# Stick-breaking attention: the causal mask moved from GpSimd, on the scores, to VectorE, where the transposed weights leave PSUM

## The chip, the cores and the metric

The kernel runs on one core of one Trainium2 chip. The metric is the device time of one execution in microseconds (us), which ends with the last instruction of the core. A core has four engines that compute: TensorE (PE in the profile, with its weight loads as PEld), VectorE (DVE), ScalarE (ACT) and GpSimd (POOL). SyncE (SP) issues the DMAs. Each engine works through its own list of instructions in order, and semaphores make it wait for the others.

## What is computed

One layer of a streaming encoder: a normalised input goes through one large projection; two mixers (stick-breaking attention and RWKV-7) read it; their outputs are projected, gated, merged and projected again. The change is in the attention, 16 heads of 64 columns, 512 prompt tokens and 8 streams of 16 new tokens:

```
def _sb_attend(q, k, v, q_pos, k_pos):
    """A[t,s] = beta[t,s] * prod_{s<j<t} (1 - beta[t,j]), beta = sigmoid(q.k/sqrt(d)), s < t only."""
    z = einsum('bhqd,bhkd->bhqk', q, k) * (D_HEAD_A ** -0.5)
    valid = k_pos[None, :] < q_pos[:, None]
    log_keep = where(valid, log_sigmoid(-z), 0.0)
    later = cumsum(log_keep, axis=3, reverse=True) - log_keep
    weight = where(valid, exp(log_sigmoid(z) + later), 0.0)
    return einsum('bhqk,bhkd->bhqd', weight, v)
```

The prompt is swept in four blocks of 128 queries; block i reads keys 0 to 128(i+1)-1. Only the last 128 keys of a block need the mask `s < t`, a 128 by 128 triangle.

## The kernel before

The matrix products of the projections are a long list of jobs of 128 output columns each (`gemm_range`). A job is two halves of eight steps, and a step is three matmuls of 320 columns (`xh·whi`, `xl·whi`, `xh·wlo`: float32 as a high and a low part). The order of jobs is: the projections that the RWKV mixer needs, mixed with those of the attention; then eight jobs for the gate gB; then eight with the weight w_o_b (called oB here), whose input is the RWKV output, reloaded into `xh` and `xl` as soon as the last gB step has read each slice (`reload`, lines 1542 to 1567: GpSimd copies a slice `xh<-rl`, VectorE forms `xl<-rl,xh`); then eight with w_o_a (oA), which needs all of the attention; then the output projection.

The attention works on eight head pairs, one after the other (`attn`, line 1294), with a preparation `aprep` of the next pair running beside it. For a pair there are nine items: the sampled streams ("s") and then, for query blocks 3, 2, 1, 0, the two heads. An item has three parts, which are staggered:

- `score`: two matmuls into a bank `ps_a`; ScalarE makes `kp` = sigmoid(-z/8) and `bt` = sigmoid(z/8); GpSimd multiplies the last 128 columns of `bt` by the triangle `see` (line 1340); VectorE scans `kp` into the running product from the right (with `stop` as the data that stands for the mask), and multiplies `bt` by it (line 1345).
- `flip`, two items later: TensorE transposes `bt` into a bank `ps_b` (two of these, shared with the transposes of `aprep`), and ScalarE copies it to `wt`.
- `pv`, once both heads of a query block are flipped: `wt` times the values into the one bank `ps_c`. For "s", the result is gated by `sg<-ps_c,sg` on VectorE, whose factor GpSimd makes (`sg<-sg,sz`), before the bank is given to the prompt's blocks.

What stands when on each engine is decided while the program is built: attention, preparation and reloads are generators, a planner (`Driver`, `Clock`, `_Eng`) keeps an estimated time for each engine, and the jobs' steps are put wherever no generator is ready by that estimate. Its costs for the two operations of this change are

```
            elif e == "dve":
                d = 0.075 + n * 0.00106
            elif e == "pool":
                d = 0.2 + n * (0.0022 if op == "tensor_tensor" else 0.0012)
```

so with n = 128 it reckons 0.48 us for the mask on GpSimd and 0.21 us for one on VectorE. A change in `score` or `flip` therefore also moves the jobs' steps.

Of the kernel before, what the change touches and what calls it, by code (L numbers as in the profile page):

```python
# [29 lines left out]
AF = mybir.ActivationFunctionType  # L30
ALU = mybir.AluOpType
# [22 lines left out]
def make_consts():  # L54
    r = np.arange(128)
    out = {}
    out["ident"] = np.eye(128)
    none = np.zeros((128, 128))
    see = (r[None, :] < r[:, None]).astype(float)
    out["see"] = see  # L60
    out["stop"] = np.concatenate([none, none, none, 1.0 - see], axis=1)
    for g in range(2):
        b = 4 * g + r[:, None] // 32
        t = r[:, None] % 16
        bb, s = r[None, :] // 16, r[None, :] % 16
        out[f"mnew{g}"] = np.where((b == bb) & (s < t), 0.0, -1e30)
    s = r[:, None] % 64
    t = r[None, :] % 64
    strict = r[None, :] < 64
    caus = np.where(strict, s < t, s <= t)  # L70
    out["maskp"] = caus.astype(float)
    out["masks"] = (caus & (s // 16 == t // 16)).astype(float)
    out["bones"] = (r[:, None] // 64 == r[None, :] // 64).astype(float)
    tok = np.arange(640)
    first = np.where(tok < 512, tok % 64 == 0, tok % 16 == 0)
    out["rmask"] = np.broadcast_to(np.where(first, 0.0, 1.0), (128, 640))
    out["msk4"] = ((r[:, None] % 64) // 16 == np.arange(4)[None, :]).astype(float)
    return np.ascontiguousarray(np.concatenate(
        [out[n] for n in CONST_COLS] + [out[n] for n in MASK_COLS], axis=1).astype(np.float32))
# [262 lines left out]
def body(tc, ins, outs, dbg=None):  # L342
# [24 lines left out]
    def take(which, *need, hold=False):  # L367


        while True:  # L370
            yield [which, *need]
            old = clk.replaced(which)
            if old not in held:
                break
            yield lambda: old not in held
        t = bank(which)
        if hold:
            held.add(_name(t))
        return t
# [16 lines left out]
    act = clk.wrap("act", nc.scalar).activation  # L396
# [25 lines left out]
    def vtt(out, in0, in1, op):  # L422
        V.tensor_tensor(out=out, in0=in0, in1=in1, op=op)

    def gtt(out, in0, in1, op):
        G.tensor_tensor(out=out, in0=in0, in1=in1, op=op)
# [867 lines left out]
    def attn(p):  # L1294
# [4 lines left out]
        stop, see = ap["msk"][:, 0:512], ap["msk"][:, 512:640]  # L1299
# [7 lines left out]
        def score(it):  # L1307
            ps = yield from take("a")
            kp = ap["as2"].tile([128, 512], F32, tag="kp", name="kp", bufs=2)
            bt = ap["as2"].tile([128, 512], F32, tag="bt", name="bt", bufs=4)  # L1310
            if it[0] == "s":
                qbd = o["qbd"]
                for g in range(2):
                    for i in range(4):
                        mm(ps[32 * i:32 * i + 32, g * 256:g * 256 + 128],
                           lhsT=qbd[:, 4 * g + i].rearrange("p h t -> p (h t)"),
                           rhs=KT[:, 4 * g + i, :], start=True, stop=True)
                    d = ps[:, g * 256 + 128:g * 256 + 256]
                    mm(d, lhsT=qbd[:, 4 * g:4 * g + 4].rearrange("p b h t -> p (b h t)"),
                       rhs=o["kT"][:, 512:640], start=True, stop=False)  # L1320
                    mm(d, lhsT=identb, rhs=mnew[g], start=False, stop=True)
                act(out=kp, in_=ps, func=AF.Sigmoid, scale=-0.125)
                act(out=bt, in_=ps, func=AF.Sigmoid, scale=0.125)
                bv = bt.rearrange("p (g s) -> p g s", g=2)
                for g in range(2):
                    c = slice(g * 256, (g + 1) * 256)
                    V.tensor_tensor_scan(out=kp[:, c][:, ::-1], data0=kp[:, c][:, ::-1],
                                         data1=stop[:, 0:256],
                                         initial=1.0, op0=ALU.mult, op1=ALU.add)
                kv = kp.rearrange("p (g s) -> p g s", g=2)  # L1330
                vtt(bv[:, :, 0:255], bv[:, :, 0:255], kv[:, :, 1:256], ALU.mult)
            else:
                _, i, h = it
                n = 128 * (i + 1)
                qs = slice(128 * i, 128 * i + 128)
                mm(ps[:, :n], lhsT=o["qh"][:, h, qs], rhs=o["ks"][:, h, :n], start=True, stop=False)
                mm(ps[:, :n], lhsT=o["ql"][:, h, qs], rhs=o["ks"][:, h, :n], start=False, stop=True)
                act(out=kp[:, :n], in_=ps[:, :n], func=AF.Sigmoid, scale=-0.125)
                act(out=bt[:, :n], in_=ps[:, :n], func=AF.Sigmoid, scale=0.125)
                gtt(bt[:, n - 128:n], bt[:, n - 128:n], see, ALU.mult)  # L1340
                kv = kp[:, :n]
                V.tensor_tensor_scan(out=kv[:, ::-1], data0=kv[:, ::-1],
                                     data1=stop[:, 512 - n:][:, ::-1],
                                     initial=1.0, op0=ALU.mult, op1=ALU.max)
                vtt(bt[:, 0:n - 1], bt[:, 0:n - 1], kp[:, 1:n], ALU.mult)
            return bt

        def flip(it, bt):
            m = 4 if it[0] == "s" else it[1] + 1
            ps = yield from take("b")  # L1350
            for i in range(m):
                tp(ps[:, i * 128:(i + 1) * 128], bt[:, i * 128:(i + 1) * 128], ident)
            wt = ap["as2"].tile([128, 512], F32, tag="wt", name="wt")
            act(out=wt[:, :m * 128], in_=ps[:, :m * 128], func=AF.Copy)
            return wt

        vt, Vp = tok["v"], o["Vp"]
# [37 lines left out]
        for n in range(len(seq) + 3):  # L1395
            if n < len(seq):
                bts[n] = yield from score(seq[n])
                if n == 0:
                    setf("sc0", p)
                if n == len(seq) - 1:  # L1400
                    setf("scored", p)
                yield []
            m = n - 2
            if 0 <= m < len(seq):
                yield [bts[m]]
                wts[m] = yield from flip(seq[m], bts.pop(m))
            m = n - 3
            if m == 0:
                yield [wts[0]]
                yield from pv(seq[0], [wts.pop(0)])  # L1410
            elif m > 0 and m % 2 == 0:
                yield [wts[m - 1], wts[m]]
                yield from pv(seq[m], [wts.pop(m - 1), wts.pop(m)])
# [366 lines left out]
```

## Time and profile before

| what | us |
|---|---|
| median of 3 runs (1156.38 to 1159.37) | 1158.27 |
| the profiled execution, its own time | 1159.46 |
| its span, first to last instruction | 1157.7 |
| busy in the span: PE | 1107.9 |
| busy in the span: DVE | 751.0 |
| busy in the span: ACT | 630.9 |
| busy in the span: POOL | 392.1 |

The attention lies between about 735 and 960 us of the span. The jobs' steps fill TensorE between its pieces, so that TensorE is busy nearly all of the time, and what the kernel can lose or gain without a change of TensorE's own work is TensorE's idle time: 1157.7 - 1107.9 = 49.8 us in the whole span. Nearly every operation is recorded by one helper line (L214), so groups are told apart by the names of their tiles.

### The profile page before, as it was taken

The numbers are of one execution on the slowest core, as the hardware profiler recorded it, in microseconds if no ns is written. First come the engines' busy times: TensorE is split into PE (matmuls) and PEld (weight loads), VectorE is DVE, ScalarE is ACT, GpSimd is POOL, SyncE is SP. The second block draws the span as 40 slices with busy tenths as digits, with TensorE's granted clock in tenths as the row PEclk, the third lists the DMA queues.
The fourth block names the chain that finished last, engine by engine and source line by source line (L and its number), as shares of the span: only waits on it lengthen the run. The fifth ranks groups of instructions, "written<-read, shape, count | busy, mean of one in ns | idle before, by whom it ended". The sixth has DMA issues, their size and how long they took to land. (4 is left out here: it accounts for less than half of the span.)

```text
span 1157.7 us, 25429 instructions
## 1 busy us (share of the span) xinstructions
PE 1107.9 (96%) x10050; PEld 1034.6 (89%) x10050; DVE 751.0 (65%) x1517; ACT 630.9 (54%) x1347; POOL 392.1 (34%) x605
## 2 busy tenths in 40 slices
PE   6999999999999999999999999998998998999997
PEld 4989899999999999899898999987887787999997
DVE  6487875855967778777783533577767775535324
ACT  5636466485595775858756465555555551123123
POOL 3030706234161361513615021445445434103302
PEclk9999999999999999999999999999999999999999
DMA  5222222233132142222323244966677525354412
GB/s 194 79 82 73 69 74 67 77 100 110 39 112 73 56 118 61 79 72 57 112 68 90 95 118 135 265 182 180 181 216 202 148 72 161 111 163 141 146 47 91
DMA packets 205294, 130.70 MB, mean 113 GB/s; under 512 B 78332, under 2 KB 184696, under 8 KB 205176
## 3 DMA queue, kind: packets, MB, share of 16 engines
q1 hardware_dynamic: 204888, 129.03, 37.9%
q8 instruction: 79, 1.29, 0.5%
q14 instruction: 39, 0.32, 0.1%
q0 software_dynamic: 288, 0.05, 0.0%
HBM read 97.70 MB, written 31.35 MB: 111 GB/s over the span
## 5 line engine op out<-in xcount | busy, mean ns | idle before, releaser
L214 PE MATMUL ps_g<-xh,whi 128*128 128x320 f32 (+1 forms) x1424 | 468.9, 329 | 1.1 <-ACT xh L214 1.1
L214 PE MATMUL ps_g<-xl,whi 128*128 128x320 f32 (+1 forms) x1424 | 443.0, 311 | 4.6 <-DVE xl L214 4.6
L214 PE MATMUL ps_g<-xh,wlo 128*128 128x320 f32 (+1 forms) x1424 | 442.2, 311 | 1.1 <-DVE wlo L214 1.1
L214 PEld LDWEIGHTS ps_g<-xh,whi 128*128 128x128 f32 x1424 | 270.5, 190 | 8.7 <-issue 3.4
L214 PEld LDWEIGHTS ps_g<-xl,whi 128*128 128x128 f32 x1424 | 270.4, 190 | 8.2 <-DVE xl L214 6.5
L214 PEld LDWEIGHTS ps_g<-xh,wlo 128*128 128x128 f32 x1424 | 269.5, 189 | 2.2 <-DVE wlo L214 2.2
L214 DVE TENSOR_TENSOR wlo<-raw,whi 128x1024 fp32r<-128x1024 f32 x97 | 123.9, 1277 | 71.3 <-ACT whi L214 70.5
L214 ACT ACTIVATE whi<-raw 128x1024 fp32r<-128x1024 f32 x97 | 102.5, 1056 | 82.3 <-PE ps_g L214 55.7
L214 DVE TENSOR_TENSOR_SCAN kp<-kp,amsk 128x256 f32<-128x256 f32 (+3 forms) x80 | 73.7, 930 | 31.6 <-ACT kp L214 31.4
L214 POOL TENSOR_TENSOR bt<-bt,amsk 128x128 f32<-128x128 f32 x64 | 44.7, 702 | 117.0 <-ACT bt L214 98.5
L214 ACT ACTIVATE kp<-ps_a 128x512 f32<-128x512 f32 (+3 forms) x72 | 33.1, 459 | 60.4 <-PE ps_a L214 31.7
L214 ACT ACTIVATE sp<-ps_g 128x320 f32<-128x320 f32 x80 | 35.0, 438 | 52.9 <-PE ps_g L214 42.6
L214 POOL TENSOR_TENSOR itmp<-INV 128x28 f32<-128x28 f32 (+6 forms) x112 | 46.5, 415 | 39.4 <-DVE INV L214 32.0
L214 ACT ACTIVATE RH<-ps_b 128x128 f32<-128x128 f32 (+1 forms) x64 | 19.4, 303 | 69.2 <-PE ps_b L214 69.0
L214 DVE SCALAR_TENSOR_TENSOR X<-ps_b,wc,SW 64x64 f32<-64x64 f32 x96 | 27.0, 282 | 45.7 <-PE ps_b L214 44.4
L214 ACT ACT_TABLE_LOAD x39 | 50.0, 1283 | 10.9 <-DVE BK L214 7.6
L214 POOL TENSOR_TENSOR wl<-wd,wh 128x256 fp32r<-128x256 f32 x8 | 7.2, 905 | 134.0 <-issue 109.1
L214 PE MATMUL ps_b<-cst,bt 128*128 128x128 f32 x192 | 33.8, 279 | 15.8 <-DVE bt L214 14.8
L214 DVE TENSOR_TENSOR bt<-bt,kp 128x511 f32<-128x511 f32 (+4 forms) x72 | 43.6, 605 | 8.2 <-POOL bt L214 0.6
L214 POOL TENSOR_TENSOR INV<-INV,itmp 128x28 f32<-128x28 f32 (+6 forms) x112 | 45.9, 410 | 8.8
L214 POOL TENSOR_TENSOR ux<-X,cst 128x256 f32<-128x256 f32 x32 | 20.3, 653 | 75.6 <-PE ps_b L214 44.7
L214 PE MATMUL ps_g<-olo,mgh 128*128 128x256 f32 x160 | 45.0, 281 | 0.0
(252 smaller groups left out, 2346.2 us busy)
## 6 DMA issues: line engine op xcount, KB each, us to landing
raw<-in_w_in_dram SPq DMA_DIRECT2D x81, 512.0 KB
q<-dr_q SPq DMA_DIRECT2D x32, 160.0 KB
Kr<-in_cache_sb_k_dram SPq DMA_DIRECT2D x16, 256.0 KB
Vp<-in_cache_sb_v_dram SPq DMA_DIRECT2D x16, 256.0 KB
raw<-in_w_o_b_dram SPq DMA_DIRECT2D x8, 512.0 KB
raw<-in_w_o_a_dram SPq DMA_DIRECT2D x8, 512.0 KB
oraw<-in_w_out_dram SPq DMA_DIRECT2D x4, 1024.0 KB
dr_zB<-zm SPq DMA_DIRECT2D x8, 320.0 KB
```

The costliest lines, as they stand in the source:

```text
L214: r = f(*a, **k)
```

## The change

The mask is taken out of `score`. In `flip`, ScalarE copies only the blocks of the transposed weights that need no mask (none for query block 0), and VectorE multiplies the last block by the transposed triangle while it moves it from PSUM to `wt`. The constant `see` is stored transposed. "s" items are as before. VectorE's scan keeps its own mask (`stop`).

```
-    out["see"] = see
+    out["see"] = see.T
...
                 act(out=bt[:, :n], in_=ps[:, :n], func=AF.Sigmoid, scale=0.125)
-                gtt(bt[:, n - 128:n], bt[:, n - 128:n], see, ALU.mult)
                 kv = kp[:, :n]
...
             wt = ap["as2"].tile([128, 512], F32, tag="wt", name="wt")
-            act(out=wt[:, :m * 128], in_=ps[:, :m * 128], func=AF.Copy)
+            if it[0] == "s":
+                act(out=wt, in_=ps, func=AF.Copy)
+            else:
+                d = slice((m - 1) * 128, m * 128)
+                if m > 1:
+                    act(out=wt[:, :d.start], in_=ps[:, :d.start], func=AF.Copy)
+                vtt(wt[:, d], ps[:, d], see, ALU.mult)
             return wt
```

So 64 GpSimd operations go (8 pairs, 8 prompt items each) and 64 on VectorE come; of ScalarE's 64 copies of prompt items, 16 go and 48 get shorter by 128 columns.

The orders of the two built programs differ in three places of interest. All are taken from the seventh pair.

VectorE, from the first item of query block 2 on (`kp<-kp,amsk` is the scan, which the profile calls TENSOR_TENSOR_SCAN; `ks<-kT,ks` belongs to the next pair's preparation). Before:

```order
L214 SCALAR_TENSOR_TENSOR kp<-kp,amsk 128x384
L214 TENSOR_TENSOR bt<-bt,kp 128x383
L214 TENSOR_TENSOR sg<-ps_c,sg 128x128
L214 SCALAR_TENSOR_TENSOR kp<-kp,amsk 128x384
L214 TENSOR_TENSOR bt<-bt,kp 128x383
L214 SCALAR_TENSOR_TENSOR kp<-kp,amsk 128x256
L214 TENSOR_TENSOR bt<-bt,kp 128x255
L214 TENSOR_TENSOR ks<-kT,ks 64x512 x2
```

The same place in the changed program:

```order
L214 SCALAR_TENSOR_TENSOR kp<-kp,amsk 128x384
L214 TENSOR_TENSOR bt<-bt,kp 128x383
L214 TENSOR_TENSOR ks<-kT,ks 64x512 x2
L214 TENSOR_TENSOR wt<-ps_b,amsk 128x128
L214 TENSOR_TENSOR sg<-ps_c,sg 128x128
L214 SCALAR_TENSOR_TENSOR kp<-kp,amsk 128x384
L214 TENSOR_TENSOR bt<-bt,kp 128x383
L214 TENSOR_TENSOR wt<-ps_b,amsk 128x128
L214 SCALAR_TENSOR_TENSOR kp<-kp,amsk 128x256
L214 TENSOR_TENSOR bt<-bt,kp 128x255
```

The mask of block 3's first head (`wt<-ps_b,amsk`) stands behind the next pair's two `ks` operations, which have moved up, and the mask of its second head behind one more scan and product.

TensorE, at the transposes of block 2's first head (`ps_b<-cst,bt 128x128 x3`), which need the product `bt<-bt,kp 128x383` above, and at block 3's `pv` (`ps_c<-wt,vtok 64x128 x8`), which needs both masks. Before:

```order
L214 MATMUL ps_b<-cst,bt 128x128 x4
L214 MATMUL ps_a<-ks,qh 128x256
L214 MATMUL ps_a<-ks,ql 128x256
L214 MATMUL ps_b<-cst,bt 128x128 x3
L214 MATMUL ps_g<-xh,whi 128x320
L214 MATMUL ps_g<-xl,whi 128x320
L214 MATMUL ps_g<-xh,wlo 128x320
L214 MATMUL ps_g<-xh,whi 128x320
L214 MATMUL ps_g<-xl,whi 128x320
L214 MATMUL ps_g<-xh,wlo 128x320
L214 MATMUL ps_c<-wt,vtok 64x128 x8
```

In the changed program four steps stand between the `ps_a<-ks,ql 128x256` and the transposes, and four between the transposes and `pv`; the last of the first four and the first of the second four are

```order
L214 MATMUL ps_g<-xh,whi 128x320
L214 MATMUL ps_g<-xl,whi 128x320
L214 MATMUL ps_g<-xh,wlo 128x320
L214 MATMUL ps_b<-cst,bt 128x128 x3
L214 MATMUL ps_g<-xh,whi 128x320
L214 MATMUL ps_g<-xl,whi 128x320
L214 MATMUL ps_g<-xh,wlo 128x320
```

Counted over the whole attention, from the first transposes of `Kr` to the last `pv`, 205 steps of the jobs stood between its pieces, and 277 do now; 88 of those with `xh` are left behind it, where 160 were. The change to the oB jobs, with its reload of `xh` and `xl`, so falls into the seventh pair's attention, where it stood behind the eighth's. TensorE's instructions are otherwise the same ones.

GpSimd, in the seventh pair, from the next pair's `ks` on. Before:

```order
L214 TENSOR_SCALAR ks<-kT 64x512 x2
L214 TENSOR_TENSOR bt<-bt,amsk 128x128
L214 TENSOR_TENSOR sg<-sg,sz 128x640
L214 TENSOR_TENSOR bt<-bt,amsk 128x128 x2
L214 TENSOR_SCALAR qh<-q_11597 128x512 x2
```

The same place in the changed program:

```order
L214 TENSOR_SCALAR ks<-kT 64x512 x2
L214 TENSOR_SCALAR qh<-q_11772 128x512 x2
L214 TENSOR_TENSOR sg<-sg,sz 128x640
L214 MEMSET qbd 128x256
L214 COPY qbd<-q_11772 64x8x16 x2
```

The pair's gate `sg<-sg,sz` now stands behind the next pair's two `qh` copies, which wait for that pair's queries from DRAM.

## Rows read from the trace of the kernel before

**Rows 1.** The page: busy time and share of each engine.

```profile
PE 1107.9 (96%) x10050; PEld 1034.6 (89%) x10050; DVE 751.0 (65%) x1517; ACT 630.9 (54%) x1347; POOL 392.1 (34%) x605
```

**Rows 2.** Windows, attention and behind: PE, PEld, DVE, ACT, POOL busy, granted clock, DMA.

```profile
735.00:960.00 225.00, 208.94 (x1906) 181.82 (x1905) 164.64 (x226) 125.47 (x297) 97.78 (x121) 0.99 0.62 173
960.00:980.00 20.00, 16.14 (x101) 15.01 (x101) 11.58 (x10) 3.64 (x6) 10.39 (x9) 0.96 0.53 168
```

**Rows 3.** Waits of PE, 735 to 960 us: total, times, longest.

```profile
PE ps_b L214 <- DVE bt L214: 14.8, 20, 2.0
```

**Rows 4.** Waits of PE, 960 to 1040 us.

```profile
PE ps_g L214 <- DVE xl L214: 3.9, 4, 2.2
```

**Rows 5.** Groups by form, DVE, 735 to 960 us: busy, mean ns, idle before.

```profile
L214 DVE TENSOR_TENSOR_SCAN kp<-kp,amsk 128x512 f32<-128x512 f32 x16 | 23.2, 1452 | 0.0
L214 DVE TENSOR_TENSOR_SCAN kp<-kp,amsk 128x384 f32<-128x384 f32 x16 | 19.2, 1197 | 0.0
L214 DVE TENSOR_TENSOR bt<-bt,kp 128x383 f32<-128x383 f32 x16 | 12.9, 804 | 1.7
L214 DVE TENSOR_TENSOR ks<-kT,ks 64x512 fp32r<-64x512 f32 x14 | 11.3, 805 | 0.3
L214 DVE TENSOR_TENSOR sg<-ps_c,sg 128x128 f32<-128x128 f32 x8 | 2.3, 285 | 8.8 <-PE ps_b L214 4.4 <-POOL sg L214 4.3
```

**Rows 6.** The same for POOL and for one form of ACT.

```profile
L214 POOL TENSOR_TENSOR bt<-bt,amsk 128x128 f32<-128x128 f32 x64 | 44.7, 702 | 117.0 <-ACT bt L214 98.5 <-issue 9.3 <-PE ps_b L214 6.2
L214 POOL TENSOR_SCALAR ks<-kT 64x512 fp32r<-64x512 f32 x14 | 16.2, 1157 | 0.8 <-DMA kT<-dr_k 0.2
L214 POOL TENSOR_TENSOR sg<-sg,sz 128x640 f32<-128x640 f32 x8 | 15.5, 1934 | 4.9 <-ACT sg L214 4.7
L214 POOL TENSOR_SCALAR qh<-q 128x512 fp32r<-128x512 f32 x14 | 13.4, 970 | 0.0
L214 ACT ACTIVATE wt<-ps_b 128x128 f32<-128x128 f32 x16 | 4.5, 279 | 9.0 <-PE ps_b L214 8.9
```

**Rows 7.** Timeline of DVE: one lone scan of the first pair, then the seventh pair.

```profile
745.58 1.21 DVE L214 TENSOR_TENSOR_SCAN kp<-kp,amsk 128x512 f32<-128x512 f32 x1
...
912.65 1.49 DVE L214 TENSOR_TENSOR_SCAN kp<-kp,amsk 128x512 f32<-128x512 f32 x1
...
917.43 1.21 DVE L214 TENSOR_TENSOR_SCAN kp<-kp,amsk 128x384 f32<-128x384 f32 x1
918.74 1.64 DVE L214 TENSOR_TENSOR bt<-bt,kp 128x383 f32<-128x383 f32 x1
...
920.50 1.00 DVE L214 TENSOR_TENSOR_SCAN kp<-kp,amsk 128x384 f32<-128x384 f32 x1
921.60 0.56 DVE L214 TENSOR_TENSOR bt<-bt,kp 128x383 f32<-128x383 f32 x1
```

**Rows 8.** Timeline of PE, seventh pair: the transposes of block 2's first head.

```profile
920.52 0.88 PE L214 MATMUL ps_b<-cst,bt 128*128 128x128 f32 x3 [1.85 <-DVE bt L214]
```

**Rows 9.** Timeline of POOL and of SP's issues, seventh pair.

```profile
914.67 2.30 POOL L214 TENSOR_SCALAR ks<-kT 64x512 fp32r<-64x512 f32 x2 [0.21 <-DMA kT<-dr_k]
917.78 2.18 POOL L214 TENSOR_TENSOR sg<-sg,sz 128x640 f32<-128x640 f32 x1
...
911.43 0.39 SPq L214 DMA_DIRECT2D kT<-dr_k  x1
911.92 2.42 SPq L214 DMA_DIRECT2D q<-dr_q  x4
```

**Rows 10.** Windows as in 2, behind two of PE's waits.

```profile
918.00:925.00 7.00, 5.15 (x37) 4.47 (x36) 6.64 (x9) 3.12 (x8) 5.08 (x5) 0.76 0.96 262
978.00:986.00 8.00, 7.43 (x30) 6.77 (x30) 7.00 (x8) 0.00 (x0) 6.96 (x7) 0.57 0.78 230
```

**Rows 11.** The chain of waits, behind the attention: start, us, what.

```profile
957.60 11.21 PE ps_g L214 x75
...
969.65 3.27 DVE xl L214 x3
```

## The prediction, made before the changed kernel was run

> **What bounds the kernel now.** I read the page first. TensorE is busy 96% of the span, no other engine more than 65% [rows 1], so the time is TensorE's work plus its idle time, and I ask which part of the idle time the change can reach. The windows show where it is: 225.00 - 208.94 = 16.1 us in the attention and 20.00 - 16.14 = 3.9 us just behind it [rows 2]. The waits by releaser say what it is made of. In the attention 14.8 us in 20 waits stand at the transposes of `bt`, for VectorE's product [rows 3]; the 3.9 us behind it are four waits of the oB jobs for `xl` [rows 4]. The rest of the idle time lies before the attention or at the end and is not touched.
>
> The attention is set by two clocks. TensorE has work for 208.94 / 8 = 26.1 us a pair, and the pairs take 225 / 8 = 28.1 us: where TensorE stands, VectorE's row of scan, product, scan, product is late. The timeline of the seventh pair shows one such place: TensorE stood 1.85 us at the transposes of block 2's first head [rows 8], for a product that ended at 918.74 + 1.64 = 920.38 [rows 7].
>
> Waits cost twice where TensorE's clock falls. Around that wait the granted clock is 0.76 over 7 us, and behind the waits for `xl` 0.57 over 8 us [rows 10], where the attention as a whole has 0.99 [rows 2]: parts of these stretches ran at 1.2 GHz in place of 2.4. The share not granted is 0.24 x 7 + 0.43 x 8 = 5.1 us.
>
> **The change, part by part.**
>
> *GpSimd's masks go:* 64 operations, 44.7 us busy [rows 6]. Nothing is gained on GpSimd itself. VectorE hardly waited for them either: its 16 products of 383 columns have 1.7 us of idle time ahead of them [rows 5]. What they cost is that VectorE runs slower beside GpSimd. The scan of 512 took 1.21 us alone and 1.49 with a mask beside it; the product of 383 took 0.56 us, and 1.64 where GpSimd made `sg` (from 917.78 on) [rows 7, 9]. Against these lone durations the means of rows 5 have an excess of 16 x (1.452 - 1.21) = 3.9 us, 16 x (1.197 - 1.00) = 3.2 and 16 x (0.804 - 0.56) = 3.9, 11.0 in all. The masks are half of the 89.8 us of the four GpSimd groups of rows 6, so my estimate is that they are worth 5.5 us of VectorE's time, with 0 and 11 as ends.
>
> *VectorE's masks come:* 64 operations from PSUM, 128 by 128. The trace has the same form in `sg<-ps_c,sg 128x128`, 285 ns [rows 5]: 64 x 0.285 = 18.2 us. Net of the above VectorE has 12.7 us more, 1.6 us a pair. ScalarE loses 16 copies of 0.279 us [rows 6] and 48 times 128 columns; it is not what TensorE waits for here, so this counts nothing.
>
> *The jobs' steps move:* 72 more of them lie inside the attention. Seventy-five matmuls, 25 steps, took 11.21 us [rows 11], so a step is 0.448 us and 72 are 32.3 us, 4.0 us a pair. They cost nothing in sum, because they are taken from behind the attention, and they cover VectorE's lateness: TensorE comes to a pair's waits 4.0 us later, VectorE 1.6 us later, and TensorE stood 14.8 / 8 = 1.85 us. In the sum every wait is covered: 1.85 + 1.6 - 4.0 is below nothing.
>
> *The places don't all agree with the sum.* I walk through the seventh pair with the new orders. TensorE is free for the transposes of block 2's first head at 920.52 - 1.85 = 918.67, and has four steps first: 920.46. VectorE's product then ended at 920.38. It should end about 1.3 us earlier, near 919.1: 0.28 from the scan of 512, 0.21 from that of 384, and some 0.8 of the 1.08 us that `sg` cost the product, since `sg` comes later now. But the transposes also need a bank, which is free only when the mask of block 3's first head has read it, and that mask now stands behind two `ks` (0.805 each) [rows 5]: 919.1 + 1.6 + 0.285 = 921.0. TensorE waits 0.5 us. Four steps on it wants block 3's `pv`, at 921.0 + 0.3 + 1.8 = 923.1, which needs the mask of the second head. VectorE must first do `sg`, and GpSimd's `sg` stands behind `qh`: with the transfers of `q` landed about 917.5 (issued until 911.92 + 2.42, plus the 3.2 us that `kT` took from issue to use [rows 9]), two `qh` of 0.970 and one `sg` of 1.934 [rows 6] end at 921.4. Then `sg` 0.285, scan 1.00, product 0.56, 0.1 between, mask 0.285: 923.6. TensorE waits another 0.5 us. Later in the pair three or four steps stand at each place, which the walk leaves without a wait. So I put 1.0 us a pair, seven pairs (the last has no next one to prepare): 7 us in place of 14.8. The ends are 0 (the sum) and 2 us a pair, 16 (GpSimd's `sg` 1 us later than I put it).
>
> *The change to the oB jobs* now shares VectorE with a pair. Before, eight `xl` ran at 3.27 / 3 = 1.09 us each with GpSimd's copies beside them [rows 11] and TensorE stood 3.9 us. Now a scan, a product and a mask stand between some of them, but TensorE has the pair's matmuls in between too. I take 5.5 us, with 0 and 9 (eight times 1.09) as ends.
>
> *The clock:* with waits of about 0.5 us in place of 1.85, I expect the first of the two slow stretches to go and the second to stay in part: 2 us back, with 0 and 5.1 as ends.
>
> Sum against the profiled execution's own time: 1159.46 - (14.8 - 7) + (5.5 - 3.9) - 2 = 1151.3 us. That execution was 1159.46 - 1158.27 = 1.2 us over the median, so the forecast is 1150 us, 0.7% below.
>
> What is late next is VectorE again, now at the masks. Queued behind a mask that waits for its transposes are the next scan and product, so TensorE's next transposes pay for it. SP's queue issues the same transfers; the jobs' weights are asked for at the start of a job, two jobs ahead, and TensorE has no wait for them in rows 3.
>
> The Trainium skill speaks against the direction of the move: Perfetto Trace Analysis, Optimizing Scalar/DVE Operations, gives VectorE about 125 ns of fixed cost on PSUM against about 51 for ScalarE, and advises to take work from a saturated VectorE. By its figures a mask on VectorE is dearer than ScalarE's copy by an estimated 74 ns, 5 us over 64. The rows show 285 against 279 ns for 128 columns, so in durations this trace doesn't agree; that VectorE is the late engine, it does.
>
> **The rivals.**
>
> *All waits go.* If GpSimd's `sg` and the bank come in time, the sum holds: 14.8 + 3.9 + 5.1 = 23.8 us at the very most, 1134.5; with the reload's wait and its clock kept, 14.8 + 2 = 17 us, about 1141. For it: 4.0 us more cover a pair, against 1.6. Against: the walk misses twice by half a microsecond.
>
> *No change.* The waits come back as long as before, at other names: 2 us a pair (16 in place of 14.8), with the reload at 5.5 and no clock gained, give 1158.3 + 1.2 + 1.6 = 1161; 1.5 us a pair give 1157. For it: the planner reckons 0.21 us for a mask that takes 0.285, and knows nothing of GpSimd and VectorE slowing each other. Against: the steps that it added are dearer than both.
>
> *Slower, because VectorE's list stands at `sg`.* GpSimd's `sg` waits behind the next pair's `ks` and `qh`, which wait for DRAM. Each microsecond that the queries land after 917.5 holds VectorE's whole list, scans and masks, by one. `sg<-ps_c,sg` already had 4.3 us of idle time for GpSimd's `sg` in eight pairs [rows 5]. The full price of the four copies is 2 x 1.157 + 2 x 0.970 = 4.25 us a pair. If the hold is 2 us a pair above my walk, TensorE waits 3 us a pair, 24 us in place of 14.8, and with the reload at 9: 1158.3 + 9.2 + 5.1 = 1172; it decides from 1.0 us a pair on, where waits of 16 us stand against 14.8. Against it: before the change GpSimd started `sg` within 6.4 us of the issue of `kT` (917.78 - 911.43), two copies and a mask ahead of it included [rows 9], so the queue of transfers is not far behind. The advice of the Trainium skill above points to this end.
>
> *The mask does nothing, the order does all.* The gain could come from the 72 steps alone; the time would be the same 1150. Only a kernel that has the steps without the mask would tell.
>
> **How the numbers follow.** Some 0.3% is what a measurement of this kernel can tell from no change, 3.5 us: 1154.8 to 1161.7. Chances: part of the waits gone, 1144 to 1154, by whichever of mask and order, 0.50; all gone, 1136 to 1144, 0.18; no change 0.14; slower 0.18, mostly 1162 to 1172. The first two are faster: 0.68. The range leaves out the fastest end of the second case and the far half of the last: 1139 to 1163. The likeliest case's own range is 1144 to 1154.
>
> **What would show each step.** In the profile after: the masks as a group of 64 on VectorE at 0.28 to 0.29 us; the scan of 512 and the product of 383 nearer to 1.21 and 0.56 us; TensorE's waits for `bt` well under 14.8 us, with new ones for VectorE's `wt` at `ps_b` and `ps_c`, near 7 us together; waits for `xl` of 4 to 7 us, now within the seventh pair; VectorE's idle time ahead of `sg` under 1 us a pair. The prediction is wrong if TensorE's waits in the attention stay at 14 us or more, or if a wait that I don't name (a weight's transfer, oA's reload behind the shorter tail of 88 steps, some 39 us) comes up.

## The result

The changed kernel took 1153.0 us (median of 5 runs, 1152.6 to 1154.1) where the kernel before took 1159.4 (1156.4 to 1161.7) beside it: a ratio of 0.9943, with a 95% interval of 0.9925 to 0.9961. It is 0.6% faster; 0.7% was forecast. The profiled execution took 1153.01 us, its span is 1151.2 us.

The page's busy time by engine for the changed kernel, which answers to [rows 1]:

```profile
PE 1104.8 (96%) x10050; PEld 1034.2 (90%) x10050; DVE 758.5 (66%) x1581; ACT 622.3 (54%) x1331; POOL 343.7 (30%) x541
```

Its windows, with the columns of [rows 2]:

```profile
735.00:960.00 225.00, 207.44 (x1820) 185.56 (x1818) 165.67 (x264) 108.87 (x256) 58.82 (x64) 0.98 0.65 178
960.00:980.00 20.00, 19.08 (x177) 16.84 (x177) 13.93 (x20) 10.34 (x21) 1.83 (x1) 1.00 0.44 122
735.00:1000.00 265.00, 246.23 (x2152) 220.65 (x2151) 193.73 (x312) 123.77 (x289) 64.92 (x71) 0.98 0.61 170
```

VectorE has 64 more instructions (1581 for 1517) and 7.5 us more to do in the whole span, GpSimd 64 fewer. TensorE is not better filled in the attention than it was: 225.00 - 207.44 = 17.6 us idle, 16.1 before. Its waits there, up to 1000 us (the attention now ends at 992), answer to [rows 3, 4]:

```profile
PE ps_b L214 <- DVE wt L214: 13.5, 9, 2.4
PE ps_g L214 <- DVE xl L214: 3.9, 2, 2.6
PE ps_b L214 <- DMA Kr<-in_cache_sb_k_dram: 1.4, 1, 1.4
```

The 14.8 us for `bt` are gone, and 13.5 us for `wt` have come. One wait of 1.4 us, for a transfer of `Kr`, is new. The waits moved more than they shrank. The gain shows a level lower, at the weight loads of the same transposes, whose waits also hold the short ones that the first list leaves out. The group of the kernel before, then of the changed one, 735 to 1000 us (busy, mean ns, idle before):

```profile
L214 PEld LDWEIGHTS ps_b<-cst,bt 128*128 128x128 f32 x192 | 22.9, 141 | 22.1 <-issue 12.2 <-ACT wt L214 5.0 <-ACT bt L214 2.4
```

```profile
L214 PEld LDWEIGHTS ps_b<-cst,bt 128*128 128x128 f32 x192 | 23.1, 142 | 17.8 <-DVE wt L214 16.0 <-issue 1.4
```

That is 4.3 us less. Of the 6.5 us by which the span fell, another 1.5 is idle time ahead of the attention (22.1 us up to 735 us before, 735 - 714.4 = 20.6 now), where the program is the same; it says nothing of the change. The stretch from 1000 us to the end, when both attentions are done, before and now:

```profile
1000.00:1157.70 157.70, 149.99 (x1111) 149.26 (x1109) 61.86 (x133) 41.68 (x79) 30.57 (x37) 0.99 0.35 114
1000.00:1151.20 151.20, 144.15 (x1075) 143.95 (x1073) 64.93 (x137) 40.63 (x78) 33.68 (x40) 0.98 0.37 120
```

At 1000 us TensorE has 36 matmuls fewer to go, some 36 x 0.149 = 5.4 us (a third of a step's 0.448 each), which bears out 4.3 + 1.5 to about 0.4 us. Behind 1000 us its idle time is 157.70 - 149.99 = 7.71 us before and 151.20 - 144.15 = 7.05 now, 0.7 us less.

VectorE's groups, 735 to 960 us, which answer to [rows 5] (seven of the eight pairs lie in this window now):

```profile
L214 DVE TENSOR_TENSOR_SCAN kp<-kp,amsk 128x512 f32<-128x512 f32 x14 | 19.1, 1365 | 0.0
L214 DVE TENSOR_TENSOR_SCAN kp<-kp,amsk 128x384 f32<-128x384 f32 x14 | 17.1, 1223 | 0.0
L214 DVE TENSOR_TENSOR wt<-ps_b,amsk 128x128 f32<-128x128 f32 x55 | 15.1, 284 | 8.8 <-PE ps_b L214 8.6
L214 DVE TENSOR_TENSOR bt<-bt,kp 128x383 f32<-128x383 f32 x14 | 12.9, 924 | 1.5
L214 DVE TENSOR_TENSOR ks<-kT,ks 64x512 fp32r<-64x512 f32 x14 | 12.4, 888 | 0.4
L214 DVE TENSOR_TENSOR sg<-ps_c,sg 128x128 f32<-128x128 f32 x7 | 2.0, 279 | 0.0
```

A mask takes 284 ns, as its nearest row said. The scans of 512 became shorter (1452 to 1365 ns), the products of 383 longer (804 to 924), and `ks` too (805 to 888). In each of the seven pairs GpSimd's `sg` now runs beside one of the VectorE operations that stand ahead of the mask: beside the product of 383 columns in four pairs, beside the scan ahead of it in one, beside a `ks` in two. The sixth pair is one of the four, VectorE and GpSimd:

```profile
908.02 1.67 DVE L214 TENSOR_TENSOR bt<-bt,kp 128x383 f32<-128x383 f32 x1
...
907.08 2.20 POOL L214 TENSOR_TENSOR sg<-sg,sz 128x640 f32<-128x640 f32 x1
```

The seventh is one of the two. VectorE, GpSimd and TensorE there, each from the timeline of its engine:

```profile
938.83 0.71 DVE L214 TENSOR_TENSOR bt<-bt,kp 128x383 f32<-128x383 f32 x1
939.57 2.65 DVE L214 TENSOR_TENSOR ks<-kT,ks 64x512 fp32r<-64x512 f32 x2
942.25 0.29 DVE L214 TENSOR_TENSOR wt<-ps_b,amsk 128x128 f32<-128x128 f32 x1
...
939.10 1.85 POOL L214 TENSOR_TENSOR sg<-sg,sz 128x640 f32<-128x640 f32 x1
...
942.60 0.44 PE L214 MATMUL ps_b<-cst,bt 128*128 128x128 f32 x2 [1.93 <-DVE wt L214]
```

The two `ks` take 2.65 us, the first of them 1.93, while GpSimd's `sg` (939.10 to 940.95) runs beside it. The mask that has to empty the bank stands behind them and ends at 942.54; TensorE, there since 942.60 - 1.93 = 940.67, waits for it.

### The profile page after: what moved, and what is told of

Read it like the earlier page. It is cut to its first block, busy times and chain, and to the rows that moved or that the text cites. A ratio compares the mean times of both kernels' runs of the same rounds, so it can differ in the third digit from the quotient of the medians.

```text
span 1151.2 us, 25308 instructions
## 1 busy us (share of the span) xinstructions
PE 1104.8 (96%) x10050; PEld 1034.2 (90%) x10050; DVE 758.5 (66%) x1581; ACT 622.3 (54%) x1331; POOL 343.7 (30%) x541
## 4 chain that ended last, share of the span: by engine, by line
PE 75%; DVE 13%; ACT 6%; DMA 3%; issue 2%; SPq 1%; POOL 0%; DVEq 0%; ACTq 0%; POOLq 0%
PE ps_g L214 52%; PE ps_a L214 10%; PE ps_b L214 8%; PE ps_c L214 5%; DVE kp L214 2%; DVE wlo L214 2%; DVE BK L214 1%; SPq L214 1%; DVE ks L214 1%; DVE xl L214 1%; ACT whi L214 1%; ACT L214 1%; DVE H L214 1%; DMA s0r<-in_state_wkv_dram 1%; ACT STG L214 1%
## 5 line engine op out<-in xcount | busy, mean ns | idle before, releaser
L214 DVE TENSOR_TENSOR_SCAN kp<-kp,amsk 128x256 f32<-128x256 f32 (+3 forms) x80 | 69.3, 874 | 40.8 <-ACT kp L214 40.7
L214 POOL TENSOR_SCALAR ks<-kT 64x512 fp32r<-64x512 f32 x16 | 14.5, 909 | 164.9 <-DMA kT<-dr_k 115.2
L214 ACT ACT_TABLE_LOAD x39 | 50.0, 1283 | 11.2 <-DVE BK L214 7.6
L214 PE MATMUL ps_b<-cst,bt 128*128 128x128 f32 x192 | 33.3, 283 | 13.5 <-DVE wt L214 13.5
L214 PE MATMUL ps_g<-ohi,mgh 128*128 128x256 f32 x160 | 45.0, 281 | 0.0
```

Of the source, the lines that this page charges most:

```text
L214: r = f(*a, **k)
```

## The experiments

All times are medians of several runs, all ratios are against the kernel before, run beside them. Two theories stood against each other. Theory 1: the jobs' steps that the planner moved into the attention are the gain, and the mask on VectorE costs part of it. Theory 2: the gain is that GpSimd no longer slows VectorE. Where an edit adds lines, an operation shows under the line it has there (L215, L1369, L1370, L1375).

### The order without the mask, and the mask without the order

The planner's bookkeeping was separated from what is issued (`plan_act`, `plan_dve` and `plan_pool` only tell the planner). First the changed kernel's orders with the work of before:

```
                 act(out=bt[:, :n], in_=ps[:, :n], func=AF.Sigmoid, scale=0.125)
+                nc.gpsimd.tensor_tensor(out=bt[:, n - 128:n], in0=bt[:, n - 128:n], in1=see, op=ALU.mult)
...
-                if m > 1:
-                    act(out=wt[:, :d.start], in_=ps[:, :d.start], func=AF.Copy)
-                vtt(wt[:, d], ps[:, d], see, ALU.mult)
+                if m > 1:
+                    plan_act(out=wt[:, :d.start], in_=ps[:, :d.start], func=AF.Copy)
+                plan_dve(out=wt[:, d], in0=ps[:, d], in1=see, op=ALU.mult)
+            nc.scalar.activation(out=wt[:, :m * 128], in_=ps[:, :m * 128], func=AF.Copy)
```

> The orders of the changed kernel on every engine (277 steps inside the attention), but the mask stays on GpSimd, on the scores, and ScalarE copies whole transposed tiles: the planner reckons with the change, the chip does the work of before. Theory 1 (the moved steps are the gain, the mask on VectorE is a cost that eats part of it): TensorE's waits for VectorE in the attention fall from 14.8 us to under 5, the time is 10 to 14 us below before, 0.988 to 0.991, and so below the changed kernel (0.9943). Theory 2 (the gain is that GpSimd no longer slows VectorE): no gain without moving the mask, 0.998 to 1.002.

Measured: 1152.7 us, 0.9927 (0.9909 to 0.9946). The first three of TensorE's waits, 735 to 1000 us:

```profile
PE ps_g L214 <- DVE xl L214: 7.6, 3, 3.2
PE ps_b L214 <- DVE bt L214: 2.4, 8, 0.5
PE ps_c L214 <- DVE sg L214: 2.3, 5, 0.8
```

The waits for `bt` fell from 14.8 to 2.4 us without any mask on VectorE: the order alone gives at least as much as the whole change. It gives less than expected (0.991 at most), and the waits at the change to oB doubled to 7.6 us. The orders of VectorE and GpSimd moved with the steps here, so this does not yet single out the steps.

Then the order of before with the changed work:

```
-                gtt(bt[:, n - 128:n], bt[:, n - 128:n], see, ALU.mult)
+                plan_pool(out=bt[:, n - 128:n], in0=bt[:, n - 128:n], in1=see, op=ALU.mult)
...
+            plan_act(out=wt[:, :m * 128], in_=ps[:, :m * 128], func=AF.Copy)
+                if m > 1:
+                    nc.scalar.activation(out=wt[:, :d.start], in_=ps[:, :d.start], func=AF.Copy)
+                nc.vector.tensor_tensor(out=wt[:, d], in0=ps[:, d], in1=see, op=ALU.mult)
```

> The orders of the kernel before on every engine (205 steps inside the attention), but the mask is done by VectorE on the way out of PSUM: the planner reckons with the kernel before, the chip does the change. Theory 1: VectorE is some 1.6 us a pair later and nothing covers it, the masks also hold a bank; TensorE's waits in the attention rise from 14.8 us to 27 to 35, the time is 10 to 20 us above before, 1.009 to 1.017. Theory 2: VectorE is no later, since GpSimd's masks are gone; 0.994 to 1.000.

Measured: 1169.8 us, 1.0075 (1.0054 to 1.0096), a little under the expected 1.009. The move by itself is a loss. TensorE's waits for the masks:

```profile
PE ps_b L214 <- DVE wt L1369: 21.6, 15, 3.0
...
PE ps_c L214 <- DVE wt L1369: 1.6, 3, 0.9
```

23.2 us, somewhat under the 27 that I expected at least, but 8.4 above the 14.8 of before. Theory 2 as a cause of the gain falls here.

### No mask at all

```
-                if m > 1:
-                    act(out=wt[:, :d.start], in_=ps[:, :d.start], func=AF.Copy)
-                vtt(wt[:, d], ps[:, d], see, ALU.mult)
+                if m > 1:
+                    plan_act(out=wt[:, :d.start], in_=ps[:, :d.start], func=AF.Copy)
+                plan_dve(out=wt[:, d], in0=ps[:, d], in1=see, op=ALU.mult)
+            nc.scalar.activation(out=wt[:, :m * 128], in_=ps[:, :m * 128], func=AF.Copy)
```

> The orders of the changed kernel, and no causal mask on the weights at all, on any engine (the scan's own mask stays; the diagonal blocks of the prompt's weights are left unmasked). ScalarE copies whole tiles. Theory 1: what is left of TensorE's waits at the transposes (13.5 us in the changed kernel, for VectorE's masks) goes, 0.987 to 0.990, 4 to 8 us under the changed kernel; against the kernel with the same orders and GpSimd's mask the difference is what GpSimd's masks cost VectorE, 0 to 4 us. Rival: the waits stay for VectorE's products, since VectorE is late by its own work, 0.992 to 0.996.

Measured: 1144.5 us, 0.9853 (0.9828 to 0.9877), lower than the 0.987 expected at least. TensorE's waits:

```profile
PE ps_g L214 <- DVE xl L214: 5.4, 3, 3.1
PE ps_b L214 <- DVE bt L214: 1.9, 4, 0.7
```

In one and the same order, the mask on GpSimd costs 0.9927 - 0.9853 = 0.7% and the mask on VectorE 0.9943 - 0.9853 = 0.9%, some 8.6 and 10.4 us. So theory 2 has a real part: GpSimd's masks do slow VectorE, and cost more than the 0 to 4 us expected. VectorE's busy time on the two pages, with GpSimd's masks (first) and without any (second), for the same 1517 instructions:

```profile
PE 1105.4 (96%) x10050; PEld 1033.8 (90%) x10050; DVE 755.1 (66%) x1517; ACT 632.4 (55%) x1347; POOL 398.3 (35%) x605
```

```profile
PE 1103.4 (97%) x10050; PEld 1033.8 (90%) x10050; DVE 743.9 (65%) x1517; ACT 631.1 (55%) x1347; POOL 345.4 (30%) x541
```

That is 755.1 - 743.9 = 11.2 us of VectorE's time. A single group can mislead. The `ks` of the same two runs:

```profile
L214 DVE TENSOR_TENSOR ks<-kT,ks 64x512 fp32r<-64x512 f32 x14 | 18.9, 1353 | 0.3
```

```profile
L214 DVE TENSOR_TENSOR ks<-kT,ks 64x512 fp32r<-64x512 f32 x14 | 12.8, 911 | 0.4
```

Much of this difference is `sg`, not the masks: it runs beside a `ks` in six of the seven pairs of the first run and in two of the second, and the products of 383, which it meets otherwise, took 640 ns in the first and 865 in the second.

VectorE's own masks cost the kernel about as much as GpSimd's, so a gain of the exchange is not shown. The 0.9943 is from another set of runs than the other two, and the intervals of the two places overlap: that one of them is cheaper is not shown either.

### What holds TensorE in the changed kernel

Three edits to the changed kernel, with its orders kept. ScalarE empties the bank and the mask follows in SBUF:

```
-                if m > 1:
-                    act(out=wt[:, :d.start], in_=ps[:, :d.start], func=AF.Copy)
-                vtt(wt[:, d], ps[:, d], see, ALU.mult)
+                if m > 1:
+                    plan_act(out=wt[:, :d.start], in_=ps[:, :d.start], func=AF.Copy)
+                plan_dve(out=wt[:, d], in0=ps[:, d], in1=see, op=ALU.mult)
+            nc.scalar.activation(out=wt[:, :m * 128], in_=ps[:, :m * 128], func=AF.Copy)
+            if it[0] != "s":
+                nc.vector.tensor_tensor(out=wt[:, d], in0=wt[:, d], in1=see, op=ALU.mult)
```

> The changed kernel with its orders, but ScalarE copies the whole transposed tile out of PSUM and VectorE multiplies its last block by the mask in place, in SBUF: VectorE does as much and in the same places, only the bank is free earlier. If TensorE waits because the mask holds the bank (13.5 us, at one of the pair's transposes, behind the next pair's two ks operations), these waits go and short ones of up to 0.5 us a pair come at pv: 1142 to 1147 us, 0.986 to 0.990. Rival: VectorE's lateness counts wherever it shows, the wait moves to pv at the same length, 0.993 to 0.996 as the changed kernel.

Measured: 1151.5 us, 0.9909 (0.9889 to 0.9930), between what I expected (to 0.990) and the rival (from 0.993), and with an interval that overlaps the changed kernel's. The waits did go as the bank said: 13.5 us at the transposes became 1.3 there and 3.7 at `pv`.

```profile
PE ps_c L214 <- DVE wt L1370: 3.7, 6, 1.8
...
PE ps_b L214 <- DVE bt L214: 1.3, 3, 0.6
```

So the bank is the wait; that freeing it gains time is not shown. That its time is not 8 us better fits a mean granted clock of 0.986 in its profile (0.990 in the changed kernel's) and a wait of 1.1 us for a weight at 1070 us that the others don't have. In its profile TensorE ran at 1.2 GHz for 13.7 us between 735 and 1000 us, where the changed kernel's has 10.2, and for another 3.4 behind that wait; at half the clock, (13.7 + 3.4 - 10.2) x 0.5 = 3.4 us more are not granted.

GpSimd's product for the gate left out:

```
-                gtt(sg, sg, sz, ALU.mult)
+                plan_pool(out=sg, in0=sg, in1=sz, op=ALU.mult)
```

> The changed kernel in its orders, with GpSimd's product of the attention's gate, eight operations of some 2.0 us, left out: the gate is the sigmoid alone, not its product with z. In the changed kernel this product runs beside VectorE's two ks operations, one of which then takes 1.93 us in place of 0.69, and the mask that holds the bank stands right behind them. If that slowing is what made the waits longer than predicted, the two ks fall to 0.7 us each in all pairs, TensorE's waits for the masks fall from 13.5 us to 3 to 6 (the prediction's own size), and the time to 1142 to 1148 us, 0.985 to 0.990. Rival: the waits come from the place of the mask alone, whatever runs beside it: they stay at 11 us or more, 0.992 to 0.995.

Measured: 1144.7 us, 0.9869 (0.9854 to 0.9884). The waits for the masks are 5.9 us, a `ks` takes 709 ns, and a product of 383 columns 592 (888 and 924 in the changed kernel):

```profile
PE ps_b L214 <- DVE wt L214: 5.9, 7, 1.2
```

```profile
L214 DVE TENSOR_TENSOR ks<-kT,ks 64x512 fp32r<-64x512 f32 x14 | 9.9, 709 | 0.4
L214 DVE TENSOR_TENSOR bt<-bt,kp 128x383 f32<-128x383 f32 x14 | 8.3, 592 | 1.5
```

Eight GpSimd operations on a side branch cost 8.6 us, 0.9943 - 0.9869: they run beside the VectorE operations that stand ahead of the mask.

The two `ks` put behind the masks:

```
-            vtt(ks[RS[1 - hh], hh], o["kT"][RS[hh], 0:TP], ks[RS[hh], hh].bitcast(F32), ALU.subtract)
+            plan_dve(**sub)
+            behind.append(sub)
...
                 vtt(wt[:, d], ps[:, d], see, ALU.mult)
+                while behind and it[2] == 1:
+                    nc.vector.tensor_tensor(**behind.pop(0))
```

> The changed kernel with one move on VectorE: the next pair's two ks operations stand behind the mask of a query block's second head, in place of ahead of the first head's; every other order stays. If the bank that the mask holds is the wait, TensorE finds the bank free (the product ends 8.6 us into the pair, the mask could follow at once, and TensorE comes at 9.7): the 13.5 us fall to 2 to 4, some of it new waits of 0.3 us at pv, and the time to 1143 to 1148, 0.986 to 0.991. Rival: VectorE is late in sum, and the ks push what stands behind them: the waits move to later transposes and stay above 9 us, 0.992 to 0.995.

Measured: 1154.6 us, 0.9947 (0.9931 to 0.9963), as the changed kernel. The rival is right. The mask now follows its product at once, but then VectorE's list stands for GpSimd's `sg`, and the `ks`, further on, delay the mask of the next block, which holds the next bank. Its sixth pair, VectorE and TensorE:

```profile
909.85 0.28 DVE L214 TENSOR_TENSOR wt<-ps_b,amsk 128x128 f32<-128x128 f32 x1
911.40 0.29 DVE L214 TENSOR_TENSOR sg<-ps_c,sg 128x128 f32<-128x128 f32 x1 [1.27 <-POOL sg L214]
...
918.35 0.28 DVE L214 TENSOR_TENSOR wt<-ps_b,amsk 128x128 f32<-128x128 f32 x1
...
918.68 0.44 PE L214 MATMUL ps_b<-cst,bt 128*128 128x128 f32 x2 [2.20 <-DVE wt L214]
```

Its waits for masks are 13.1 us in all, 13.5 in the changed kernel. In this exchange it did not count which operation stands ahead of the mask: VectorE was late either way.

### Telling the planner

If steps are what covers VectorE, the planner should be told what VectorE's products cost. From the attention on, in the changed kernel:

```
                 d = 0.075 + n * 0.00106
+                if self.clk.told and op == "tensor_tensor":
+                    d = 0.15 + n * 0.00125
```

> The changed kernel with dearer VectorE products in the planner's estimate, from the attention on (0.15 + 0.00125 n us in place of 0.075 + 0.00106 n); the work on the chip is the same, 335 steps stand inside the attention in place of 277, and 30 behind it in place of 88. If moved steps are what covers VectorE, the waits fall from 13.5 us to under 4 and the time to 1143 to 1150, 0.986 to 0.992. Rival: the cover is used up, since oB's reload then lies deeper in the attention and oA's reload has only 30 steps, 13 us, to hide behind: waits for xl or oA of 8 us or more, 0.995 to 1.003.

Measured: 1145.6 us, 0.9876 (0.9863 to 0.9889).

```profile
PE ps_g L215 <- DVE xl L215: 7.5, 2, 5.7
PE ps_b L215 <- DVE wt L215: 3.6, 6, 1.0
```

The waits for masks are 3.6 us in place of 13.5. The reload of oB costs 3.6 us more, as the rival feared, but not as much as is won. The same lines in the kernel before, its mask on GpSimd:

> The kernel before, mask on GpSimd, with the same dearer VectorE products in the planner's estimate as in the run of the changed kernel that was told of them; 231 steps stand inside the attention in place of 205. If the moved steps are the gain and the place of the mask is not, it is faster than before without the change: 26 steps of 0.448 us, 11.6 us of cover, against 14.8 us of waits for bt: these fall to 3 to 7 us, 1148 to 1153 us, 0.990 to 0.995. Rival: the mask on VectorE is needed for the gain, since with it on GpSimd VectorE is slowed in the same places; 0.997 to 1.001.

Measured: 1145.2 us, 0.9881 (0.9867 to 0.9895), better than expected.

```profile
PE ps_b L215 <- DVE bt L215: 4.4, 6, 1.1
PE ps_g L215 <- DVE xl L215: 3.5, 4, 2.2
```

This comes nearest to the steps alone. Without the jobs' and the reload's own operations, VectorE's row in the attention has 212 operations, of which 204 keep the order of the kernel before, and GpSimd's has 121, of which 118 do; 26 more steps took the waits for `bt` from 14.8 to 4.4 us.

And the changed kernel told of it, with ScalarE emptying the bank:

```
-                if m > 1:
-                    act(out=wt[:, :d.start], in_=ps[:, :d.start], func=AF.Copy)
-                vtt(wt[:, d], ps[:, d], see, ALU.mult)
+                act(out=wt[:, :m * 128], in_=ps[:, :m * 128], func=AF.Copy)
+                vtt(wt[:, d], wt[:, d], see, ALU.mult)
```

> The changed kernel with the dearer products in the planner's estimate, and with the bank freed by ScalarE: it copies the whole transposed tile, and VectorE masks the last block in place in SBUF. The planner knows that the bank is free earlier and puts 277 steps inside the attention, 88 behind it. If both causes are removed at once (the bank held by a late mask, and VectorE reckoned too cheap), waits in the attention stay under 5 us and the reload of oB, not being deeper than in the changed kernel, costs 4 us: 1142 to 1148, 0.984 to 0.990. Rival: the mask in SBUF has two inputs there and takes 0.315 us or more beside GpSimd's copies, and pv waits for it: 0.990 to 0.995.

Measured: 1142.6 us, 0.9873 (0.9854 to 0.9892). The first two of its waits:

```profile
PE ps_g L215 <- DVE xl L215: 3.7, 3, 2.5
PE ps_b L215 <- ACT wt L215: 2.7, 3, 1.7
```

These three can't be told apart. All beat both the kernel before and the changed one by more than their intervals, and they have the mask in three different places. The last one has no more steps in the attention than the changed kernel, 277: in its first seven pairs `sg` slows none of the products of 383 and `ks` (640 and 707 ns in the mean of all pairs), and ScalarE frees the bank. How much of its gain is either was not separated.

## Why the prediction was right, and where it was not

**The direction and its cause were right.** The order carries the gain: the order alone gives 0.9927, the mask alone 1.0075. That the steps in it do so is borne out by the kernel before that was told: 26 steps were reckoned as 11.6 us of cover, and 10.4 us of waits went. The rival "the mask does nothing, the order does all" was put beside the forecast with the same time, 1150; it is the better account, and the mask does less than nothing without the order.

**The masks' price was right, GpSimd's was too low.** 64 masks at 284 ns were forecast at 285. For what GpSimd's masks cost VectorE I took 5.5 us with 11 as the upper end; the two runs in one order give 11.2 us of VectorE's time, and some 8.6 us of the kernel's. So VectorE did not have 12.7 us more to do, but 7.5. Nor was it 1.6 us a pair later: without the order the waits rose by 23.2 - 14.8 = 8.4 us, some 1.1 a pair.

**The step that was mis-sized is the walk, "1.0 us a pair, seven pairs: 7 us in place of 14.8".** It measured 13.5 us. The place was right: 11.2 of the 13.5 us stand in six of the seven pairs at the transposes of block 2's first head, waiting for the bank that block 3's mask had to empty, 1.9 us each where the walk had 0.5. In the third pair TensorE had already stood the 1.4 us for `Kr`. In the seventh TensorE came 9.74 us after the pair's first scan (940.67 - 930.93) and the walk had 9.79; the mask was late, and ended 11.6 us after that scan where the walk had 10.3.

The term that failed is VectorE's row ahead of the mask. I took 0.8 us off the product because `sg` comes later, and priced the two `ks` by their mean before, 2 x 0.805 = 1.6 us. But in four pairs `sg` still lay beside the product, 1.67 to 1.87 us in place of 0.56; in one beside the scan of 384, 2.33 in place of 0.95; in two beside a `ks`, 1.93, so that the two took 2.65 us in the seventh pair. With `sg` left out the waits are 5.9 us. The walk's own figures showed this: it had `sg` on GpSimd from 919.5 to 921.4 and the two `ks` on VectorE from 919.1 to 920.7, and used the collision only as a gain. The second half of the walk, 0.5 us at `pv`, did not come; that the first wait was long enough to cover it is argued, not shown.

**The change to oB** cost 3.9 us, as before; 5.5 was forecast, and it did move into the seventh pair. I had read 1.09 us for an `xl` off the chain; their mean was 1.27 before, and is 0.92 now (735 to 1000 us, before and now):

```profile
L214 DVE TENSOR_TENSOR xl<-rl,xh 128x640 fp32r<-128x640 f32 x8 | 9.7, 1267 | 2.1 <-POOL xh L214 2.1
```

```profile
L214 DVE TENSOR_TENSOR xl<-rl,xh 128x640 fp32r<-128x640 f32 x8 | 7.0, 917 | 0.0
```

**The clock** gave nothing back, 2 us were forecast. Over 735 to 1000 us TensorE ran 10.2 us at 1.2 GHz before (920.3 to 923.7 and 978.3 to 985.1), and 10.2 now:

```profile
784.50:787.90 3.40, 3.01 (x12) 3.01 (x13) 3.16 (x9) 0.85 (x3) 0.00 (x0) 0.50 0.74 242
849.40:852.80 3.40, 3.40 (x21) 3.07 (x21) 3.25 (x8) 0.85 (x1) 0.00 (x0) 0.50 0.57 157
955.20:958.60 3.40, 3.40 (x20) 3.07 (x17) 3.29 (x9) 0.72 (x3) 0.72 (x1) 0.50 1.01 297
```

These stand at or just behind waits of 2.4, 2.0 and 2.6 us, two of them for masks.

**The sum came near in part by luck.** The 8.2 us forecast were 6.4 (1159.46 - 1153.01 by the profiled executions). Two terms fell short by 6.5 and 2, and the reload won 1.6 against its forecast. Waits too short for the list that I read fell by some 3 us (4.3 at the weight loads, 1.3 of it in the list), on which I hadn't reckoned; the idle time ahead of the attention was 1.5 us shorter, which is not the change's doing, and that behind 1000 us 0.7: 8.2 - 6.5 - 2 + 1.6 + 3 + 1.5 + 0.7 = 6.5. I had set two signs for a wrong prediction. Waits of 14 us or more in the attention: those for the masks are 13.5, and 14.9 with the 1.4 for `Kr`. A wait that I don't name: that for `Kr` is one. So in the waits the mechanism did worse than the time.

**The rivals.** "No change" was right about the listed waits, which came back at other names, 13.5 us for 14.8, though not about the time. "VectorE's list stands at `sg`" did not happen: idle time ahead of it is 0.0 us in seven pairs. It came in the run with the `ks` behind the masks, at 1.27 us in a pair, so the price was real and the two `ks` ahead of it hid it. "All waits go" did not happen in the changed kernel. With 335 steps those for masks fell to 3.6 us, but those at the reload rose to 7.5.

## What to carry to other kernels

Where a planner writes the order from estimated costs, a change of an operation is two changes, and they can be run apart: issue the new work in the old order and the old work in the new one. Here the move by itself cost 0.75%, the order it brought gained 0.7%, and better estimates gained 1.2% with the mask in any of three places.

An operation that empties a PSUM bank and stands in the list of the late engine makes TensorE wait for that list: 13.5 us here, and 5.0 once ScalarE emptied it. What that is worth in time was not shown (0.9943 and 0.9909, with overlapping intervals). An operation that is moved takes its collisions along: ask what it will run beside after the move.

## What the hardware showed

A VectorE operation with both inputs in SBUF lost about as long as GpSimd's product beside it still had to run: the first `ks` ran from 939.57 to 941.50, GpSimd's `sg` ended at 940.95, and a `ks` without it takes 0.71 us. The Trainium skill says so (SBUF — State Buffer, Summary: rules for kernel authors: of a VectorE instruction with two SBUF inputs and a GpSimd instruction that reads SBUF, the one that issues second waits until the first has finished), and this trace agrees to about 0.2 us: 940.95 + 0.71 = 941.66, measured 941.50. In all seven pairs the operation beside `sg`, the scan of 384 included, ended within 0.2 us of the end of `sg` plus its own lone time.

The Trainium skill also says (SBUF — State Buffer, Who interferes with whom) that a VectorE instruction with at most one SBUF input, outside the modes that use both ports, is free of it. This trace agrees: the masks from PSUM took 284 ns in the mean and 294 at most. Of the 64 with both inputs in SBUF, whose mean is 315, one took 1.66 us and one 0.80:

```profile
L1370 DVE TENSOR_TENSOR wt<-wt,amsk 128x128 f32<-128x128 f32 x64 | 19.5, 315 | 9.9 <-ACT wt L1368 9.7
```
